# A mixture of softmaxes: the last 64 columns of one batch stored in small row groups, from 15 rows down to 1 and then 8, on the load queue

## The chip, the cores and the metric

One core of a Trainium2 chip. The metric is device time in microseconds (us), the median over the runs of a kernel. A profiled run also gives a "span", which is 1 to 2 us shorter than the timed run.

The change makes sixteen row groups: 15, 14, ... 1 is fifteen, and then one of 8 (120 + 8 = 128 rows).

## The reference, cut to what matters

```python
batch, seq, vocab, num_heads = 32, 128, 4096, 4       # logits [32,128,4,4096], prior [32,128,4], f32
prior_probs = softmax(prior, axis=-1)                   # [32, 128, 4]
mixture = sum_h prior_probs[..., h, None] * softmax(logits[:, :, h, :], axis=-1)   # [32, 128, 4096]
```

Each batch reads 8.39 MB of logits and writes 2.10 MB of output. Rows are the 128 partitions.

## The kernel before

The parts that matter: two buffers for loads, two for the result `acc`, all loads on the sync engine's queue ("load queue", q1 in the profile), nearly all stores on the scalar engine's queue ("store queue", q10).

```python
lpool = ctx.enter_context(tc.tile_pool(name="lpool", bufs=2))
apool = ctx.enter_context(tc.tile_pool(name="apool", bufs=2))
# ...
def load(b):                                             # n = 4 heads at once until the last three batches
    lt = lpool.tile([P, H, V], FP32, name="ltile")
    n = pieces(b)
    for h in range(0, H, n):
        nc.sync.dma_start(out=lt[:, h : h + n], in_=logits[b, :, h : h + n, :])
    ltiles[b] = lt

def store(b, lo=0, hi=V, eng=nc.sync):
    eng.dma_start(out=out[b, :, lo:hi], in_=accs[b][:, lo:hi])
# ...
for b in range(B):
    # ...
    if 0 < b < B - 3:
        store(b - 1, eng=nc.scalar)
    # ...
    for h in range(H):
        # ScalarE: et = exp(lt[:, h]), row sums in dsum; VectorE: coeff = prior / dsum
        # VectorE: acc = et * coeff (h == 0), else acc = et * coeff + acc
    if b + 2 < B:
        load(b + 2)                                      # waits for ScalarE to have read batch b
```

So load 23 is issued at the end of iteration 21, and the store of batch 20 at the start of iteration 21.

The softmax here doesn't subtract the row's maximum and nothing guards it: scores larger than these inputs give would overflow.

## Time and profile before

| | before |
|---|---|
| time, median (2 runs) | 784.72 us (784.62 to 784.82) |
| span of the profiled run | 782.8 us |
| one batch in the steady state | 24.18 us |
| HBM traffic | 335.6 MB, 429 GB/s |
| load 23 issued / load 22 landed | 544.30 / 551.41 us |

Lines of the profile's page before: the busy table, then the DMA queues (packets, MB, share of the span of 16 engines).

```profile
DVE 544.9 (70%) x408; ACT 472.7 (60%) x258; POOL 0.2 (0%) x4
...
q1 hardware_dynamic: 6624, 276.83, 82.0%
q10 hardware_dynamic: 4080, 58.79, 17.5%
q14 instruction: 8, 0.07, 0.0%
HBM read 268.50 MB, written 67.11 MB: 429 GB/s over the span
```

VectorE and ScalarE have slack. Queue q14, which the page calls `instruction`, moves 8 packets of 8,192 B in the span. The load and store queues together keep the 16 DMA engines busy for 99.5% of the span, so DMA time is the time of the kernel.

Stretches of the kernel before, one for each of three iterations (columns: stretch, its length, busy time of VectorE, ScalarE and GpSimd with instruction counts, clock, DMA share, GB/s):

```profile
527.33:551.51 24.18, 16.83 (x12) 14.72 (x8) 0.00 (x0) 1.00 1.00 434
551.51:576.14 24.63, 16.83 (x12) 14.73 (x9) 0.00 (x0) 1.00 1.00 431
576.14:600.31 24.17, 16.82 (x12) 14.73 (x9) 0.00 (x0) 1.00 1.00 434
```

DMA share 1.00 throughout. A load packet of 65,536 B takes 2,418 ns, and 16 engines at that pace make 16 x 65,536 B / 2.418 us = 433.7 GB/s; these stretches move 431 to 434. At this packet time nothing is left to gain from the DMA engines here. That their idle time is lost is shown by the changed kernel: 4.5 us of it and 1.6 us of slow packets, less 0.4 us of idle at the end, went with a span 5.6 us longer.

The timeline before around load 23 (columns: start, us, engine, line, operation; in brackets the idle time before it and what ended it):

```profile
544.30 0.33 SPq L45 DMA_DIRECT2D ltile<-in_logits_dram  x1
...
551.51 3.62 ACT L100 ACTIVATE etile<-ltile 128x4096 f32<-128x4096 f32 x1 [7.24 <-DMA ltile<-in_logits_dram]
551.62 0.34 ACTq L51 DMA_DIRECT2D out_dram<-acc  x1
```

Load 23 is issued 7.1 us before load 22 lands and iteration 22 starts. Its packets stand in the queue when load 22's last ones leave, so the load queue never runs dry: in the packet records at least 2 load packets run at each moment looked at from 30 to 690 us (every 0.05 us).

The packet records show how the two queues share: an engine sends one 65,536 B load packet (2,418 ns), then one 16,384 B store packet (611 ns), in turn, and one such round takes 3.03 us. Eight rounds make a batch (8 x 3.03 = 24.2 us against 24.18). The trace does not number the engines; the turns are read from the times: of the load packets that start between 100 and 690 us, 88% end within 20 ns of the start of a store packet, and 88% of the store packets end so near the start of a load packet.

The 16 engines are not in step. Each load has 16 landings and 16 packets of 4 B, which I take for one of each per engine. I call the time from the first to the last of the 16 landings of one load its spread. It was 0.71 us for the first load, 2.62 us at the third, 2.36 us at load 22 and 2.81 us at load 23. The slowest engine decides when a load has landed: ScalarE began on load 22 at 551.51 us, after the last of its landings (551.41), though 15 of the 16 were in at 550.88.

### The profile page before, as it was taken

The page shows a single profiled execution, that of the slowest core. Times are in us where ns is not written, and L with a number is a line of the kernel's source. Part 1 is how long each engine was busy: PE and PEld are TensorE (multiplying, and loading weights), DVE is VectorE, ACT ScalarE, POOL GpSimd, SP SyncE. Part 2 cuts the span into 40 slices and gives each one's busy share as a digit, 9 for nine tenths or more (in the row PEclk, how much of TensorE's full clock was granted, in tenths as well). Part 3 has the DMA queues.
Part 4 walks back from the last instruction along what each step waited for, and adds up shares of the span by engine and source line. Part 5 has one row for each costly group of instructions (what it writes and reads, how often), then busy time and mean ns, then how long its engine had stood idle before and what let it go on. Part 6 is the DMA issues. An engine that isn't in the chain of part 4 may idle for free.

```text
span 782.8 us, 977 instructions
## 1 busy us (share of the span) xinstructions
DVE 544.9 (70%) x408; ACT 472.7 (60%) x258; POOL 0.2 (0%) x4
## 2 busy tenths in 40 slices
DVE  3576687666786667866678666687666876669994
ACT  0766556755567555575555765556755567558971
POOL 0000000000000000000000000000000000000000
DMA  9999999999999999999999999999999999999997
GB/s 378 429 429 448 416 454 411 456 410 457 423 417 445 447 424 442 433 424 435 422 450 422 444 423 448 419 447 419 453 414 455 421 422 443 440 414 429 428 429 334
DMA packets 10712, 335.68 MB, mean 429 GB/s; under 512 B 1200, under 2 KB 1200, under 8 KB 1232
## 3 DMA queue, kind: packets, MB, share of 16 engines
q1 hardware_dynamic: 6624, 276.83, 82.0%
q10 hardware_dynamic: 4080, 58.79, 17.5%
q14 instruction: 8, 0.07, 0.0%
HBM read 268.50 MB, written 67.11 MB: 429 GB/s over the span
## 4 chain that ended last, share of the span: by engine, by line
DMA 73%; DVE 18%; ACT 6%; issue 1%; DVEq 0%; ACTq 0%
DMA ltile<-in_logits_dram 39%; DMA out_dram<-acc 34%; DVE acc L108 10%; ACT etile L100 6%; DVE ltile L108 3%; DVE acc L106 3%; DVE ltile L106 1%; DVE coeff L104 1%; DVE ltile L114 0%; DVE rden L103 0%; DVEq L152 0%; ACTq L100 0%; ACTq L51 0%; DVEq L106 0%
## 5 line engine op out<-in xcount | busy, mean ns | idle before, releaser
L100 ACT ACTIVATE etile<-ltile 128x4096 f32<-128x4096 f32 x120 | 433.4, 3612 | 276.3 <-DMA ltile<-in_logits_dram 203.9
L108 DVE SCALAR_TENSOR_TENSOR acc<-etile,coeff,acc 128x4096 f32<-128x4096 f32 x90 | 403.6, 4484 | 3.2
L103 DVE RECIPROCAL rden<-dsum 128x1 f32<-128x1 f32 x128 | 20.2, 158 | 156.3 <-ACT etile L100 156.3
L106 DVE TENSOR_SCALAR acc<-etile,coeff 128x4096 f32<-128x4096 f32 x30 | 70.6, 2353 | 50.1 <-DMA out_dram<-acc 50.0
L100 ACT ACTIVATE ltile<-ltile 128x4096 f32<-128x4096 f32 x8 | 28.9, 3610 | 4.8 <-DMA ltile<-in_logits_dram 2.2
L104 DVE TENSOR_TENSOR coeff<-rden,pp 128x1 f32<-128x1 f32 x128 | 20.4, 159 | 4.4
L108 DVE SCALAR_TENSOR_TENSOR ltile<-ltile,coeff 128x4096 f32<-128x4096 f32 x5 | 22.4, 4485 | 0.2
L100 ACT ACTIVATION_READ_ACCUMULATOR etile<-ltile 128x1 f32 x120 | 22.4, 186 | 0.0
L60 DVE TENSOR_REDUCE pmax<-pr 32x128 f32<-32x512 f32 x1 | 0.7, 673 | 11.5 <-DMA pr<-in_prior_dram 11.5
L64 ACT ACTIVATE pe<-pc 32x512 f32<-32x512 f32 x1 | 0.6, 628 | 10.4 <-DVE pc L62 10.4
L114 DVE SCALAR_TENSOR_TENSOR ltile<-ltile,coeff 128x1024 f32<-128x1024 f32 x4 | 4.9, 1281 | 0.0
L106 DVE TENSOR_SCALAR ltile<-ltile,coeff 128x4096 f32<-128x4096 f32 x2 | 4.7, 2353 | 0.1
L64 ACT ACT_TABLE_LOAD x1 | 1.3, 1283 | 1.2 <-PEq L141 1.2
L78 DVE STREAM_TRANSPOSE pp<-pn 32x32 f32<-32x32 f32 x16 | 1.9, 170 | 0.1
L100 ACT ACTIVATION_READ_ACCUMULATOR ltile<-ltile 128x1 f32 x8 | 1.5, 186 | 0.0
L66 DVE TENSOR_REDUCE psum<-pe 32x128 f32<-32x512 f32 x1 | 0.7, 674 | 0.7 <-ACT pe L64 0.7
L71 DVE TENSOR_TENSOR pn<-pe,prec 32x512 f32<-32x512 f32 x1 | 1.0, 1021 | 0.0
L68 DVE RECIPROCAL prec<-psum 32x128 f32<-32x128 f32 x1 | 0.9, 942 | 0.0
L62 DVE TENSOR_TENSOR pc<-pr,pmax 32x512 f32<-32x512 f32 x1 | 0.7, 678 | 0.0
L141 POOL MEMSET const-bfloat16-1.0<- 128x1 bf16 x1 | 0.1, 101 | 0.0
L141 POOL MEMSET const-uint8-127<- 128x1 uint8 x1 | 0.1, 101 | 0.0
L141 POOL MEMSET const-float32-0.0<- 128x1 f32 x1 | 0.1, 98 | 0.2 <-issue 0.2
(1 smaller groups left out, 0.1 us busy)
## 6 DMA issues: line engine op xcount, KB each, us to landing
out_dram<-acc ACTq DMA_DIRECT2D x28, 2048.0 KB, 30.0
ltile<-in_logits_dram SPq DMA_DIRECT2D x12, 2048.0 KB, 22.9
out_dram<-acc SPq DMA_DIRECT2D x2, 2048.0 KB, 34.1
out_dram<-ltile SPq DMA_DIRECT2D x1, 2048.0 KB, 22.8
out_dram<-ltile SPq DMA_DIRECT2D x2, 1024.0 KB, 10.2
ltile<-in_logits_dram SPq DMA_DIRECT2D x29, 31.3
pr<-in_prior_dram ACTq DMA_DIRECT2D x1, 64.0 KB, 10.7
```

Of the source, the lines that this page charges most:

```text
L60: nc.vector.reduce_max(pmax, pr, axis=AX.X)
L62: nc.vector.tensor_sub(pc, pr, pmax.unsqueeze(2).to_broadcast([B, S, H]))
L64: nc.scalar.activation(pe, pc, AF.Exp)
L68: nc.vector.reciprocal(prec, psum)
L71: nc.vector.tensor_mul(pn.rearrange("b h s -> b s h"), pe, prec.unsqueeze(2).to_broadcast([B, S, H]))
L78: nc.vector.transpose(pp[32 * t : 32 * (t + 1), h, :], pn[:, h, 32 * t : 32 * (t + 1)])
L100: nc.scalar.activation(et, lt[:, h], AF.Exp, accum_out=dsum)
L103: nc.vector.reciprocal(rden, dsum)
L104: nc.vector.tensor_mul(coeff, rden, pp[:, h, b : b + 1])
L106: nc.vector.tensor_scalar_mul(out=acc, in0=et, scalar1=coeff)
L108: nc.vector.scalar_tensor_tensor(out=acc, in0=et, scalar=coeff, in1=acc, op0=ALU.mult, op1=ALU.add)
L114: nc.vector.scalar_tensor_tensor(out=acc[:, cs], in0=et[:, cs], scalar=coeff, in1=acc[:, cs], op0=ALU.mult, op1=ALU.add,)
```

## The change

The intent seems to be to change how the engines stand to each other: a group of n rows lands in n parts (10 landings for the 10 rows of the 6th small store), by the prediction one for each engine that it uses, so a staircase of row groups may be meant to give some engines a little more than others. Which engines these would be is not shown. The bytes and the arithmetic stay.

```diff
--- before.py
+++ after.py
@@ -80,6 +80,8 @@
             )
 
     NCHUNK = 4
+
+    CUT, CUTW = 20, 64
     CW = V // NCHUNK
 
     for b in range(B):
@@ -87,7 +89,16 @@
         inplace = b >= B - 2
         lt = ltiles.pop(b)
         if 0 < b < B - 3:
-            store(b - 1, eng=nc.scalar)
+            whole = b - 1 != CUT
+            store(b - 1, hi=V if whole else V - CUTW, eng=nc.scalar)
+            if not whole:
+                lo = 0
+                for n in [*range(15, 0, -1), 8]:
+                    nc.sync.dma_start(
+                        out=out[CUT, lo : lo + n, V - CUTW :],
+                        in_=accs[CUT][lo : lo + n, V - CUTW :],
+                    )
+                    lo += n
         if not inplace:
             accs[b] = apool.tile([P, V], FP32, name="acc")
         else:
```

## The prediction

> **What bounds the kernel now.** The DMA engines. The queue table shows them busy 82.0% + 17.5% of the span, at 429 GB/s. A 65,536 B load packet takes 2,418 ns, so 16 engines can move 433.7 GB/s[...]. In the steady state one batch (8.39 MB in, 2.10 MB out) takes 24.18 us in the timeline, which is that rate. VectorE (70%) and ScalarE (60%) have slack. Each load is issued about 7.1 us before the previous one lands, so the load queue never runs dry. In the tail stores queue up to the end, so DMA time lost anywhere shows in full.
>
> **What the change moves.** No arithmetic, no bytes. (The list has sixteen groups: 15 to 1 is fifteen, then 8.) Batch 20's store goes from 16,384 to 16,128 B a row; 32 KB go as 128 rows of 256 B on the sync queue. [...] In the trace the landings of one DMA already spread over 2.4 us[...]. I expect nothing from that: 16 such packets are 0.15 us at the packet rate, perhaps 0.5 us with overhead (estimate).
>
> **Where it costs.** The sync queue is in order, and the built program has eight DMA completion semaphores in rotation: each DMA waits until the one eight places earlier has landed. Load 22 comes before the sixteen stores, load 23 after them. The 7th store reuses load 22's semaphore, the 8th that of batch 20's main store, the 9th to 16th those of the 1st to 8th. So the sync queue stops until load 22 has landed (T, about 551.4 us), where before load 23 was issued at 544.3 us. After T: 7th store at T+0.1, 8th when the main store has landed (about T+1.3, the load queue being empty), then nine issues at 0.48 us (back-to-back spacing in the tail): load 23 at about T+5.6, its first packets 1.0 to 1.7 us later (as the trace's first load): T+7. The load queue is dry for 7 us.
>
> **How much is lost.** The store queue fills most of it. Left of the main store is about one packet (0.6 us). Batch 21's store now waits for the 4th small store, which sits behind load 22: issue about T+1.5, data T+2.5, 8 packets x 0.611 = 4.9 us, until T+7.4. True idle: T+0.9 to T+2.5, perhaps 0 to 1 us more before load 23, plus 0.3 us of small packets. VectorE's first write of batch 22 waits for the 16th small store, about 2 us later than before, absorbed by slack. Load 23 then runs without a competing store (8 x 2.418 = 19.3 us); load 24 is issued in time. A one-time loss of about 2.6 us, kept to the end.
>
> **Predicted: 787.3 us, range 785.6 to 790.5.** Faster by over 2%: 1%; within 2%: 97%; slower: 2%.
>
> **What would show it.** Load 23's issue at T+5.6 instead of T-7.1; sync's waits on load 22 and the main store; no load packet for 7 us, store packets back to back inside; one iteration of about 27 us, the next ones 24.18 again; landings of 15, 14, ... 1 engines.
>
> **What would make it wrong.** 256 B writes taking microseconds (more loss); sync issuing small stores much slower than 0.48 us; or the pause removing the 2.4 us spread (gain).

## The result, and the profile after

| | before | after |
|---|---|---|
| time, median (2 runs each) | 784.72 us | 790.28 us (790.19 to 790.36) |
| ratio | | 1.0067, 95% interval 1.0043 to 1.0091 |
| span | 782.8 us | 788.4 us |
| load 22 landed (T) | 551.41 us | 550.82 us |
| load 23 issued | T - 7.1 us | T + 7.4 us |
| iterations 22, 23, 24 | 24.62, 24.17, 24.18 us | 30.03, 26.12, 24.18 us |

A ratio is the mean time of one kernel's fast runs over that of the other's of the same rounds, so it is not quite the ratio of the medians. The change costs 5.6 us, 0.7%: inside 2%, and clear of the noise. A second set of four runs (first experiment) gave 790.15 us.

The page after:

```profile
DVE 545.3 (69%) x408; ACT 472.1 (60%) x258; POOL 0.2 (0%) x4
...
q1 hardware_dynamic: 6880, 276.86, 81.6%
q10 hardware_dynamic: 4080, 58.75, 17.4%
...
HBM read 268.50 MB, written 67.11 MB: 426 GB/s over the span
```

There are 256 more packets on the load queue: 128 of data (256 B) and 128 of 4 B, by their number one for each landing of data. Their own duration is small: the records show 18 ns and 9 ns, together 128 x 27 ns / 16 = 0.2 us on the average of the engines. The bytes of HBM are the same. The loss is not the work of the small stores.

The sync queue's own waits after (what waited for what: us in total, times, longest):

```profile
SPq L45 <- ACT etile L111: 495.1, 29, 19.3
...
SPq L97 <- DMA ltile<-in_logits_dram: 16.9, 1, 16.9
...
SPq L97 <- DMA out_dram<-acc: 6.3, 2, 5.3
```

A small store (L97) waits 16.9 us for a load: it is the 7th, for load 22. Of the 6.3 us for stores, 5.3 are the 6th small store waiting for the store of batch 19 (which landed at 533.61 us, long before load 22), and 1.0 the 8th waiting for the main store of batch 20. The timeline after shows what that holds up; first the sync queue alone, then the same stretch with the other engines (a fence for each, since they merge lines differently; the second is put together from short windows):

```profile
526.21 31.90 SPq L97 DMA_DIRECT2D out_dram<-acc  x16
558.21 13.40 SPq L45 DMA_DIRECT2D ltile<-in_logits_dram  x2
```

```profile
550.84 0.28 SPq L97 DMA_DIRECT2D out_dram<-acc  x1
550.93 3.62 ACT L111 ACTIVATE etile<-ltile 128x4096 f32<-128x4096 f32 x1 [6.28 <-DMA ltile<-in_logits_dram]
552.19 1.29 SPq L97 DMA_DIRECT2D out_dram<-acc  x4
552.80 0.34 ACTq L51 DMA_DIRECT2D out_dram<-acc  x1
...
557.17 0.95 SPq L97 DMA_DIRECT2D out_dram<-acc  x1
558.05 0.19 ACT L111 ACTIVATION_READ_ACCUMULATOR etile<-ltile 128x1 f32 x1
558.21 0.69 SPq L45 DMA_DIRECT2D ltile<-in_logits_dram  x1
560.28 2.35 DVE L117 TENSOR_SCALAR acc<-etile,coeff 128x4096 f32<-128x4096 f32 x1 [5.26 <-DMA out_dram<-acc]
```

The sixteen small stores occupy the sync queue from 526.21 to 558.1 us. The 7th is issued at 550.84, when load 22 has landed; the 8th at 552.19, when batch 20's main store has. The reason lies in the built program, whose semaphores the trace gives: it has eight completion semaphores for DMAs (99, 100 and 103 to 108) and hands them out in turn, and a DMA that takes one over first waits until the earlier DMA on it has landed. The 7th small store takes over that of load 22 (104: the last landing on it is at 550.82 us, the store is issued at 550.84), the 8th that of the main store (105: 552.17 and 552.19). Load 23 comes after all sixteen.

What the DMA engines did meanwhile, in stretches of 2 us, before and then after (a packet counts in the stretch in which it starts, so a share can exceed 1 or fall below it for one stretch; read the run of them):

```profile
549.00:551.00 2.00, 1.04 (x1) 0.00 (x0) 0.00 (x0) 1.00 1.25 541
551.00:553.00 2.00, 0.00 (x0) 1.49 (x1) 0.00 (x0) 1.00 1.25 541
553.00:555.00 2.00, 0.00 (x0) 2.00 (x1) 0.00 (x0) 1.00 1.04 451
555.00:557.00 2.00, 0.32 (x2) 2.00 (x3) 0.00 (x0) 1.00 0.53 229
557.00:559.00 2.00, 1.46 (x1) 1.82 (x2) 0.00 (x0) 1.00 1.34 582
```

```profile
549.00:551.00 2.00, 1.42 (x1) 0.07 (x1) 0.00 (x0) 1.00 0.45 178
551.00:553.00 2.00, 0.00 (x0) 2.00 (x1) 0.00 (x0) 1.00 0.04 12
553.00:555.00 2.00, 0.30 (x2) 2.00 (x3) 0.00 (x0) 1.00 0.79 330
555.00:557.00 2.00, 0.03 (x1) 2.00 (x1) 0.00 (x0) 1.00 1.09 459
557.00:559.00 2.00, 0.00 (x0) 1.23 (x2) 0.00 (x0) 1.00 0.64 265
```

From 551 to 553 us the engines moved 12 GB/s. By the packet records no load or store packet of full size runs from 551.6 to 553.7 us; then the store of batch 21 runs alone (8 packets on each engine, one straight after the other) until 558.8; then there is a second gap until load 23's first packets at 559.5 to 560.2 us. In the two gaps together all engines lack such packets for 2.8 us. The last engine lost about 3 us (an estimate, since the trace does not number the engines), and the others more: they had been up to 2.15 us ahead and had nothing left to do.

There is a second part. The first load packet of each engine after the pause took 2,604 to 3,496 ns in place of 2,418, and when the next store joined, most load packets were slow for some 30 us: of the 174 that start between 579 and 611 us, 134 took over 2,440 ns, up to 2,899. Before, two load packets over 2,440 ns occur in the whole stretch from 545 to 640 us, and each of these starts 0.3 us after an instruction packet of q14 (at 562.6 and 613.4 us): they take 2.95 and 2.67 us. No run tested whether that is the cause.

To add this up for every run I used the packet records: idle is the length of a stretch minus the sum of all packets' durations over 16 (packets overlap by a few ns, so a stretch that is always busy shows -0.3 us in 95); slow-packet time is, over 16 too, the sum of each packet's duration minus the usual one for its size (2,418, 611 and 601 ns for 65,536, 16,384 and 16,128 B). Both are averages over the engines. The differences to before, in us:

| run (profiled) | load 23 issued | span | idle, 545 to 640 us | slow packets, 545 to 640 us | idle after 700 us |
|---|---|---|---|---|---|
| after | T + 7.4 | +5.6 | +4.5 | +1.6 | -0.4 |
| staircase_again | T + 7.4 | +5.3 | +4.3 | +1.5 | -0.6 |
| equal16 | T + 7.6 | +5.6 | +4.1 | +1.6 | -0.3 |
| six_groups | T + 0.1 | +3.9 | +1.8 | +1.9 | -0.1 |
| held_landing | T + 0.3 | +3.9 | +2.3 | +1.7 | -0.3 |
| held_4us | T + 4.1 | +3.1 | +1.5 | +1.6 | -0.5 |
| held_7us | T + 7.7 | +4.0 | +4.6 | +1.5 | -2.0 |
| held_7us_again | T + 7.7 | +4.1 | +4.5 | +1.5 | -1.9 |
| equal24 | T + 10.2 | +8.0 | +8.1 | +1.8 | -2.1 |
| five_groups | T - 7.1 | +1.1 | -0.1 | 0.0 | +0.9 |
| four_groups | T - 7.0 | +0.6 | 0.0 | 0.0 | +0.2 |
| four_a_batch | T - 7.0 | +0.1 | -0.1 | 0.0 | +0.2 |

The rest of each row (0.5 us at most) lies mostly at the start of the kernel, which differs from run to run. This table is an account of one profile each, not an intervention. The run of experiment 8, which is not in it, has 22.8 us of slow packets. The experiments in the rows are told next.

### The profile page after: what moved, and what is told of

Read it like the earlier page. It is cut to its first block, busy times and chain, and to the rows that moved or that the text cites. A ratio compares the mean times of both kernels' runs of the same rounds, so it can differ in the third digit from the quotient of the medians.

```text
span 788.4 us, 993 instructions
## 1 busy us (share of the span) xinstructions
DVE 545.3 (69%) x408; ACT 472.1 (60%) x258; POOL 0.2 (0%) x4
```

## The experiments

The theory: load 23 is late because the small stores in front of it reuse the semaphore of load 22; the DMA engines then stand idle, and start again slowly. Rivals: the staircase itself, that is uneven packets over the engines; or the small stores as such, by number or by their 256 B writes. Each experiment's "before" was timed in the same rounds: 784.82 us in the first group of four, 784.85 in the second, 784.67 in the third; each group ran on another chip. Results were correct in all.

### 1. The changed kernel once more

No edit; it stands beside the next three on one chip.

> The changed kernel once more, beside the others on one chip. Both theories: 790.0 to 790.6 us, load 23 issued about 7.4 us after load 22 landed.

790.15 us, ratio 1.0068 (1.0053 to 1.0083). Load 23 was issued at 558.37 us, 7.4 us after load 22 landed at 550.94. As expected. The spread took another course than in the first profile of this kernel: 2.23, 2.44, 1.40, 2.37 us at loads 22 to 25, where it had been 2.15, 1.15, 2.23, 2.10. The loss is the same, so the course of the spread does not decide it here.

### 2. Sixteen equal groups

```diff
-                for n in [*range(15, 0, -1), 8]:
+                for n in [8] * 16:
```

> Sixteen small stores of 8 rows each in place of the staircase: same number of DMAs, same semaphores reused, same bytes[...]. Theory A (the late load 23 costs, the staircase is nothing): 789.5 to 791 us, load 23 issued 6.5 to 8 us after load 22 landed, and the spread of landings again falls to under 1.2 us and grows back to about 2.3. Rival B (the staircase of packets over the engines costs): clearly under 788 us.

790.33 us, ratio 1.0068 (1.0053 to 1.0083), the same as the staircase. Load 23 was issued 7.6 us after T. The staircase is not the cause: sixteen equal groups cost as much. (Each equal group has eight rows, and the stores of 8 rows in the changed kernel had eight landings of data; that the staircase as such costs nothing that can be resolved is shown by experiment 9, ratio 1.0001.) The spread did not do quite what I wrote: 2.05 us at load 22, 2.55 at load 23, 1.43 at load 24, 2.73 at load 25.

### 3. and 4. Six groups and four groups

```diff
-                for n in [*range(15, 0, -1), 8]:
+                for n in [16, 16, 16, 16, 32, 32]:      # six_groups
+                for n in [8, 4, 4, 112]:                # four_groups
```

With six, load 23 itself takes over load 22's semaphore. With four it takes over that of load 21, which landed long before.

> Six small stores of 16, 16, 16, 16, 32, 32 rows. Load 23 now reuses load 22's semaphore itself, so it is issued when load 22 lands (7 us later than before) but not behind ten more small stores. Theory A1 (only the time in which an engine has no packet counts): idle of about 1 us on the last engine, so 785.4 to 786.2 us. Theory A2 (a pause of both queues also puts the 16 engines in step, and they lose about 2 us more until they are spread again): spread of landings under 1.2 us after the pause, 16 engines' load packets over 2,440 ns for some 30 us, and 786.7 to 788.2 us. Rival B (cost is per small store): 5.6 x 6/16 = 2.1 us, 786.8, but with load 23 late or not alike.

> Four small stores of 8, 4, 4 and 112 rows: no semaphore of load 22 or later is reused before load 23. Theory A: load 23 issued on time, 7 us before load 22 lands; 784.5 to 785.1 us, like before. Rival C (256 B writes or the cut rows of the main store cost): over 786 us. [...]

Six groups: 788.07 us, ratio 1.0039 (1.0022 to 1.0055). Four groups: 785.16 us, ratio 1.0001 (0.9986 to 1.0016), not resolved from before, though the median is a little above what I had given. So 256 B writes and a cut main store cost nothing that can be seen. The six cost 3.3 us, which only the theory with a slow restart (A2) had in its range among the two forms of A; the rival by number (B) was 1.3 us too low. Within A2, the slow packets were there (1.9 us) but the spread did not fall under 1.2 us: it was 2.25 at load 22 and 2.48 at load 23.

The sync queue's timeline of six_groups: load 23 is issued at 551.49, just after load 22 landed at 551.42.

```profile
525.96 7.69 SPq L97 DMA_DIRECT2D out_dram<-acc  x6
551.49 0.36 SPq L45 DMA_DIRECT2D ltile<-in_logits_dram  x1
```

In four_groups, the first store of 4 rows has four landings of data, and the last of them (553.06 us) stands 1.10 us after the one before it; the last of the main store's 16 landings (552.87) stands 1.03 us after the one before. So the late engine seems to be among the four that this store used. The trace does not number the engines.

### 5. No small store at all: load 23 held until load 22 has landed

From the kernel before. The added operation reads one element of batch 21's tile, so load 23, which overwrites that tile, must wait for it; and it reads one element of batch 22's, so it waits for load 22.

```diff
+    gate = cpool.tile([1, 1], FP32, name="gate")
...
+        if b == 21:
+            nc.gpsimd.tensor_add(gate, lt[0:1, 0, 0:1], ltiles[22][0:1, 0, 0:1])
         if b + 2 < B:
             load(b + 2)
```

> The kernel before with no small store at all; one POOL operation on one element, which reads batches 21 and 22, holds load 23 until load 22 has landed (T), so it is issued at about T+0.4 instead of T-7. Theory A (the late load is the cost, and the restart in step is part of it): 786.5 to 788.3 us, like the six groups; spread of landings under 1.2 us or 15 or more load packets over 2,440 ns after the pause. If only the idle of the last engine counted: 785.2 to 785.9. Rival B (cost is per small store): 784.5 to 785.2.

788.15 us, ratio 1.0044 (1.0029 to 1.0059), within what theory A gave. This is the decisive run: 3.3 us are lost with no small store in the program, as much as with the six groups. The timeline shows the hold and the late issue:

```profile
552.00 0.18 POOL L122 TENSOR_TENSOR gate<-ltile 1x1 f32<-1x1 f32 x1 [551.56 <-DMA ltile<-in_logits_dram]
552.07 0.34 ACTq L52 DMA_DIRECT2D out_dram<-acc  x1
552.21 0.33 SPq L45 DMA_DIRECT2D ltile<-in_logits_dram  x1
```

Only for 0.2 us (552.7 to 552.9) does no engine have a load or store packet, and the time is above what counting the last engine's idle alone had given (785.2 to 785.9), so that falls.

### 6. and 7. Held longer: 7 us, and the same kernel again for a second profile

```diff
+            if (b, h) == (22, 1):
+                nc.gpsimd.tensor_add(gate, lt21[0:1, 0, 0:1], dsum[0:1, :])
+                load(23)
...
-        if b + 2 < B:
+        if b == 21:
+            lt21 = lt
+        elif b + 2 < B:
             load(b + 2)
```

> As held_landing, but load 23 is held by the second exponential of batch 22, so it is issued about 7.3 us after load 22 landed, as in the changed kernel (7.4), while the store of batch 21 is not held back. Theory A: 789.0 to 790.7 us, i.e. most of the 5.5 us with no small store in the program. Rival B: 784.5 to 785.5. The dose between held_landing and this one: 7 us later at issue costs only 2 to 3 us more, because the store of batch 21 (4.9 us at full rate) fills the rest.

> The same kernel as held_7us, for a second profile: does the spread of landings stay under 1 us until the end again, without slow packets after 580 us? If it does, engines in step are not slow by being in step, and the pause decides whether the spread comes back. If the spread grows to over 2 us this time, it is chance from run to run. Time 788.4 to 789.2 either way.

788.70 us, ratio 1.0051 (1.0036 to 1.0066), and 788.72 in the single run. That is 3.9 us of the 5.5, less than I expected. The idle, averaged over the engines, is as large as in the changed kernel (4.6 and 4.5 us), though the first gap is shorter (here 551.9 to 552.5 and 557.7 to 559.7 us), because the store of batch 21 is not held back and so also ends sooner. The difference lies after it: in the changed kernel the spread grew back, to 2.23 us at load 24 and 2.72 at load 26. Here it stayed at 0.5 to 0.95 us to the end in both profiles (but for one quarter of load 29, 1.26 us), and no run of slow packets came after 580 us. The table shows it as 2.0 us less idle at the end: no engine has to be waited for there. So part of what the pause takes comes back if the engines stay together.

This also corrects me. I had taken it that engines in step are slow until they are apart again. These two profiles show engines within 1 us of each other and, between 580 us and the last three batches, a single slow packet.

### 8. Eight engines restarted out of step with the other eight

From experiment 5, load 23 in three DMAs:

```diff
+        for lo, hi in [(0, 8), (16, 128), (8, 16)] if b == 23 else []:
+            nc.sync.dma_start(out=lt[lo:hi], in_=logits[b, lo:hi])
...                                                      # the loop over h is skipped for b == 23
```

> As held_landing, but load 23 goes in three DMAs: rows 0 to 7 (8 engines), rows 16 to 127 (16 engines), rows 8 to 15 (8 engines), so eight engines restart 2.4 us out of step with the other eight[...]. Theory of the step (16 engines in the same phase slow each other): far fewer load packets over 2,440 ns between 555 and 625 us than in held_landing, under a third of the added packet time. Rival D (any restart after a pause is slow for some 30 us): as many as in held_landing. Total 787 to 791 us either way[...]: the packets decide, not the total.

810.91 us, ratio 1.0334 (1.0318 to 1.0349): inconclusive for its question, and instructive for another. The split made the packets slow itself (held_landing, the same kernel without it, took 788.15 us), so it says nothing about being in step. That 8 rows take eight engines is read from the eight landings of data of the changed kernel's 8-row stores; which eight is not shown. The first eight 65,536 B packets (rows 0 to 7) took 7.1 to 9.0 us each in place of 2.418, and those of rows 16 to 127, which follow, 2.7 to 7.2 us. The stretch of that load in the profile:

```profile
553.00:595.00 42.00, 16.91 (x12) 12.85 (x8) 0.00 (x0) 1.00 1.08 273
```

273 GB/s with the engines full (DMA share 1.08): they were busy, but slow. No run tested why, and I have not worked it out, neither for rows 0 to 7 nor for rows 16 to 127.

### 9. The same sixteen small stores, four in each of four batches

The 64 columns are copied to a tile of their own first, so that the stores need not come at once. The cut is against the changed kernel and leaves out the lines that set up `tail`, `done` and `STEPS` (the sixteen sizes).

```diff
             if not whole:
-                lo = 0
-                for n in [*range(15, 0, -1), 8]:
-                    nc.sync.dma_start(...)              # from accs[CUT]
+                nc.vector.tensor_copy(out=tail, in_=accs[CUT][:, V - CUTW :])
+            if CUT < b <= CUT + 4:
+                for n in STEPS[4 * (b - CUT - 1) : 4 * (b - CUT)]:
+                    nc.sync.dma_start(out=out[CUT, done : done + n, V - CUTW :], in_=tail[done : done + n, :])
+                    done += n
```

> The same staircase of sixteen small stores, but from a copy of the 64 columns and four in each of four batches, so that no load waits for a load: every load is still issued about 7 us early. Theory A: 784.6 to 786.0 us[...]. Rival B (the staircase itself or the number of small stores costs 5.5 us): 789 us or more.

784.77 us against 784.85, ratio 1.0001 (0.9984 to 1.0018). The whole staircase, with the same sixteen DMAs, costs nothing that can be resolved once no load waits behind it. The sync queue's timeline: load 23 is issued at 543.73, 7.0 us before load 22 lands, ahead of the second four.

```profile
525.55 1.91 SPq L101 DMA_DIRECT2D out_dram<-tail  x4
543.73 0.37 SPq L45 DMA_DIRECT2D ltile<-in_logits_dram  x1
550.76 5.48 SPq L101 DMA_DIRECT2D out_dram<-tail  x4
```

### 10. Five groups: one fewer than six

```diff
+                for n in [16, 16, 32, 32, 32]:
```

> One small store fewer than six_groups (16, 16, 32, 32, 32 rows). Load 23 then reuses the semaphore of batch 19's store, which landed long before. Theory A (reuse of load 22's semaphore): load 23 again issued 7 us before load 22 lands, no slow packets, 784.5 to 785.3 us. If the cost grew smoothly with the number of small stores: 787.5.

785.04 us against 784.67, ratio 1.0006 (0.9991 to 1.0021). The threshold lies between five and six, where the built program's semaphores put it, and not in a smooth cost per store:

```profile
526.50 3.02 SPq L97 DMA_DIRECT2D out_dram<-acc  x5
544.94 0.36 SPq L45 DMA_DIRECT2D ltile<-in_logits_dram  x1
```

The five do not quite leave the engines alone: the spread in this profile went from 3.0 to 5.1 us in two batches, so the last engine lost time, some of which came back by the end. The other two kernels with small stores and a load on time also show a wider spread from load 23 on (four_groups 2.3 to 3.9 us, four_a_batch 1.9 to 3.2; before, 2.4 to 2.8). The timed runs do not resolve a cost in any of the three.

### 11. Twenty-four groups

```diff
+                for n in [8] * 8 + [4] * 16:
```

> Twenty-four small stores (eight of 8 rows, sixteen of 4). The 20th reuses the semaphore of batch 21's store, which lands about 8.5 us after load 22 (T); load 23 follows at T+10.5 to T+12. The store of batch 21 is done by then, so each further us is idle for all engines. Theory A: 792.5 to 795.5 us. If only the restart cost, however long the pause: 790.

791.79 us, ratio 1.0090 (1.0073 to 1.0107): more than sixteen, but less than I expected. Load 23 was issued 10.2 us after T. Idle rose by 8.1 us and the slow packets stayed at 1.8 us, so the slow packets cost about the same at T + 10.2 us as at T + 0.1 (six_groups, 1.9 us). As in held_7us the spread stayed under 1 us to the end (but for 1.68 us at one quarter of load 29), and there was 2.1 us less idle at the end; I had not counted that.

### 12. Held 4 us

As experiment 6, with `(b, h) == (22, 0)`.

> As held_7us, but load 23 is held by the first exponential of batch 22: issue at about T+3.8, while the store of batch 21 (4.9 us at full rate from about T+1.2) is still moving. No second gap, so idle of the last engine about 0.7 us as in held_landing; 787.0 to 788.4 us, at or under held_7us (788.7).

787.25 us, ratio 1.0032 (1.0017 to 1.0047), as expected. Load 23 was issued 4.1 us after T, while the store of batch 21 was still moving, and there was no second gap. A later issue did not cost more here, while the other queue had work: the median is even 0.9 us under that of held_landing, which was timed in other rounds and on another chip.

## Why the prediction was right, and where its size was off

The time fell within the range (790.28 us; 785.6 to 790.5), near its upper end. The loss was predicted as about 2.6 us and was 5.6. The mechanism of the late load was right, but the sum of its cost lacked a term, and that the wide range still held the time, with 0.2 us to spare, is partly luck.

- **The bound.** Right. The DMA engines set the time (the two queues take 99.5% of the span before), VectorE and ScalarE have slack (70% and 60% busy), and idle DMA time shows in full (with the slow packets 5.7 us on the average of the engines, against 5.6 of span).
- **The staircase itself does nothing that can be resolved.** Shown by equal16 (790.33 us against 790.15) and four_a_batch (784.77 against 784.85). By the packet records sixteen 256 B packets with their 4 B packets take 16 x 27 ns = 0.43 us.
- **Sixteen small stores hold load 23 by reuse of semaphores.** Shown: the issue moved from T - 7.1 to T + 7.4 us, the waits that hold the sync queue from load 22's landing on are the two that were named (a third, 5.3 us for the store of batch 19, was over before), five groups do not hold it and six do, and held_landing loses as much as six groups with no small store in it. (Not quite as predicted, the 12th to 16th took over the semaphores of the 5th to 9th, since batch 21's store took that of the 4th.)
- **How the small stores use the engines.** By the number of landings as predicted: the store of 14 rows has fifteen semaphore updates, one of them 0.6 us after its issue (527.30 us) and the other fourteen from 550.40 us on, and the store of 7 rows has eight, the first 0.5 us after its issue and the other seven from 1.1 us after it on. What the early one stands for, and which engines the rows use, is not shown.
- **"nine issues at 0.48 us: load 23 at about T+5.6".** Mis-sized: T + 7.4. The 7th to 12th stores took 0.28 to 0.30 us each to issue, but the last four took 1.06, 1.03, 1.08 and 0.95 us. They were issued while the store of batch 21 ran at full rate. Busy engines alone are not the reason: the first five were issued with all 16 engines busy (16 load and store packets run at each moment looked at from 526.2 to 528.4 us, every 0.2 us) and took 0.34 to 0.44 us. The reason was not tested.
- **"True idle: T+0.9 to T+2.5, perhaps 0 to 1 us more".** A little small: the gaps of the last engine are 551.6 to 553.7 and 558.8 to about 559.8 us, 3 us together (estimate), where the prediction had 1.6 to 2.6.
- **What was missing from the sum.** The restart. Load packets after the pause were slower, by 1.6 us on the average of the engines. With 4.5 us of idle on that average and 0.4 us less idle at the end this makes 5.7 us, against 5.6 measured. The spread was 2.15 us before the pause and 2.1 us in the last batches, so the last engine lost in all about what the average lost. All seven kernels of the table whose load 23 came late have 1.5 to 1.9 us of slow packets, and the three whose load came on time have none. The prediction held the opposite to be possible: that the pause would close the spread and so gain. It did close it in held_7us and equal24, which have 2 us less idle at the end, but not for long in the changed kernel.
- **"one iteration of about 27 us, the next ones 24.18 again".** 30.03, then 26.12, then 24.18. Of the 1.9 us of the second long one, 0.9 us are slow packets (between 576 and 612 us, averaged over the engines); the rest goes with the spread, which grew from 1.15 to 2.23 us there. In the second profile of this kernel the landings of loads 23, 24 and 25 follow by 31.5, 23.7 and 24.7 us.
- **VectorE's first write of batch 22, "about 2 us later".** It began 9.5 us after T instead of 6.1, so 3.3 us later; absorbed, since load 24 was issued at 571.25 us, 9.6 us before load 23 landed.

What stays open: why packets are slow for a while after a pause, and why the spread grows back after some pauses and not after others. Being in step is not enough (experiments 6 and 7), and the run that was to separate phase from restart spoiled itself.

For the spread the traces hold a lead that no run tested: the instruction packets. In the thirteen profiles other than that of experiment 8, each q14 packet between 90 and 690 us that comes while loads run is followed within 0.6 us by a load packet of 2.66 to 3.02 us, so one engine falls back by 0.2 to 0.6 us. In held_7us, held_7us_again and equal24, and in no other profile, the q14 packet of this stretch (at 557.7, 557.4 and 561.5 us) falls into the pause, where there is no load to hold up. These are the three in which the spread fell to 0.5 to 0.6 us and stayed low; in the other six with a late load it was 1.15 us or more at load 23.

Slow packets also occur at the start, when the first load and later the first store begin: before, all 48 load packets that start in the first 10 us took over 2,440 ns (up to 3,538), and 51 of the 110 that start between 48.7 and 70 us; after, 48 of 50 and 40 of 110. That is a likeness and not an explanation.

## What to carry to other kernels

A queue's order is a dependency. Before putting extra DMAs ahead of a load, count them against the completion semaphores of the built program, and see which earlier DMA each of them must wait for: five small stores cost nothing that the timed runs resolve (0.4 us), and six cost 3.3 us, because the sixth pushed the load onto a semaphore that was still in use.

Where DMA is the bound, keep each queue's next transfer issued before the last one ends. Here a pause of the load queue cost idle time (1.5 to 8.1 us on the average of the engines) and a restart besides (1.5 to 1.9 us, whether the load was 0.1 or 10.2 us late), even where the other queue filled most of the gap.
